# A hybrid decoder layer on one core: turned query and key rows split over all 128 partitions, and half of the second weight unit loaded into exponential tiles

## The chip, the core and the metric

The kernel runs on one core of one Trainium2 chip. The core has a matmul engine (PE, with its weight loads PEld), a vector engine (DVE), an activation engine (ACT), a general engine (POOL) and a queue that issues nearly all of this kernel's DMAs (SP). The metric is the device time of one launch in microseconds (us), lower is better; the median of several executions counts.

## What is computed

One decoder layer on x of 1 x 1024 x 1024 float32. The parts that matter here, shortened:

```python
h = rms_norm(x, norm1_w)
da_q, da_k, da_v, dn_qkv, dn_z, dn_a, dn_b = split(h @ w_in)
da_q = rms_norm(da_q.reshape(B, S, 4, 2, 64), q_norm_w)   # 4 heads, two maps of 64 each
da_k = rms_norm(da_k.reshape(B, S, 4, 2, 64), k_norm_w)
a = softmax(q1 @ k1.T) - lam * softmax(q2 @ k2.T)         # causal, per head
da_o = rms_norm(a @ v, da_out_norm_w) * (1 - lam_init)
dn_o = gated_delta_rule(conv_silu(dn_qkv), ...)           # 4 heads, chunked scan
x = x + concat(da_o, dn_o) @ w_out
x = x + square(relu(rms_norm(x, norm2_w) @ w_up)) @ w_down
```

## The kernel before the change

Every matmul of float32 data is made of two parts: a rounded high part (fp32r) and the low rest, and three products high x high, high x low, low x high. A weight block is therefore loaded as float32 (`raw`), rounded on ACT (L213) and its rest made on DVE (L214).

The launch runs in stages. To about 220 us come the first norm, the gate columns and the convolution stage of the DeltaNet heads. From there to about 620 us one stage mixes many streams: the blockwise inversion (`horner`), the chunked `scan` with its outputs (`scan_out`), the projections of the attention heads (`da_units`), the turning of normed queries and keys (`da_turns`), the attention itself (`scores`, `values`), the turning of its outputs and the output projection. Then the MLP runs to the end.

In the mixed stage the PE's order is written out by a planner (`Interleave`): every stream is a generator that says when its next piece can run by a table of costs (`act`, `vec`, `DMA_T`, `unit_time`), and the planner emits the piece of highest priority that is due. PE keeps that order to the letter. The order of ACT, DVE, POOL and SP is made by the tile framework's scheduler from the same program; each engine then works through its own list strictly in turn, and so does SP.

The pieces that the change and the prediction touch:

- `load_unit` (L199) loads one weight block after another. In the attention stage a half unit has four blocks, k = 0 to 3, of 128 x 512; each is two DMAs of 128 KB (L211), a rounding on ACT (L213) and a rest on DVE (L214). The float32 blocks go through a ring of two buffers (`wraw`), so the load of k = 2 stands behind the rest of k = 0.
- `da_units` (L987) has three units (512 columns each) by eight row tiles. A unit has two halves of the contraction, `kh` 0 and 1. Two row tiles share a turn: four k-groups of three matmuls (L1012 to L1014) for each tile with `kh` 0, then four for each with `kh` 1. The sums stand in two PSUM banks (`ps_qk`), one for each of the two tiles. `leave` drains a bank with one ACT instruction (`qn`, L1040; in the second unit L1034 and L1035). The next half unit's weights are loaded when the last pair has used the old ones, as the staged buffers `wH` and `wL` come in two pairs.
- `da_turns` (L956) turns 256 normed columns of one row tile: two PE transposes into `ps_qkt` (L965, L966), then high and low part. Partitions 0 to 63 of the turned tile hold the rows of map one, 64 to 127 those of map two. For each map m, ACT rounds the 64 partitions into `qa[a, m]` (L972) and DVE writes the rest into the other 64 partitions, `qa[b, m]` (L973). One DMA stores `qa` to `qk_d` (L977). There are 32 turns, two buffers of `qa`.
- `load_head` (L1064) loads a head's keys, one tile for each map (L1068), 512 KB each, 128 partitions. `load_q` (L1081) loads a query tile twice: `qa` as stored (L1085, 128 KB) and `qb` with the halves of the partitions exchanged (L1086, L1087, 64 KB each), so that two matmuls (L1148, L1149) give all four products of high and low parts.
- `horner` (L781) works in four tiles of the pool `ae` (tag `pexp`, four buffers): two named `gb`, two named `pb`. Later `scores` writes its exponentials into tiles of the same tag. DVE reads `gb` for the last time in the transposes behind L800.

What sets the order of the load of weights: the ring `wraw` for the raw blocks, the last reader of `wH` and `wL` on PE, and the place of each DMA on SP.

Of the kernel before, what the change touches and what calls it, by code (L numbers as in the profile page):

```python
# [9 lines left out]
F32 = mybir.dt.float32  # L10
# [109 lines left out]
def act(n, accum=False):  # L120
    return "S", 55.0 + 0.83 * n + (93.0 if accum else 0.0)


def vec(n, extra=0.0):
    return "V", 68.0 + 1.045 * n + extra
# [7 lines left out]
def tile_hymba_layer(  # L133
# [62 lines left out]
    hH = hpool.tile([P, KB, SEQ], F32R, name="hH")  # L196
    hL = hpool.tile([P, KB, SEQ], F32R, name="hL")

    def load_unit(src, ranges, k0=0, nk=KB, eng=None, rp=None):  # L199
        eng = eng or G  # L200
        width = sum(n for _, n in ranges)
        wh, wl = staged("wH"), staged("wL")
        wh = wh[:, :nk * width].rearrange("p (k c) -> p k c", k=nk)
        wl = wl[:, :nk * width].rearrange("p (k c) -> p k c", k=nk)
        st = 2 * UC // width
        for k in range(0, nk, st):
            raw = rp.tile([P, 2 * UC], F32, tag="wraw", name="wraw", bufs=5) if rp else laid("wraw")
            raw = raw[:, :st * width].rearrange("p (k c) -> p k c", k=st)
            o = 0
            for c0, n in ranges:  # L210
                nc.sync.dma_start(raw[:, :, o:o + n], src[:, k0 + k:k0 + k + st, c0:c0 + n])  # L211
                o += n
            S.copy(wh[:, k:k + st, :], raw)  # L213
            eng.tensor_tensor(wl[:, k:k + st, :], raw, wh[:, k:k + st, :].bitcast(F32), ALU.subtract)  # L214
        return wh, wl
# [552 lines left out]
    HF = (slice(0, 64), slice(64, 128))  # L768
    MM, TR = 219.0, 110.0

    def unit_time(eng="G", rate=1230.0):
        done = []
        for i in range(4):
            start = flow.now if i < 2 else done[i - 2]
            done.append(flow.chain(("S", 520.0), (eng, rate), start=start + DMA_T))
        return done

# [179 lines left out]
    def da_turns():  # L957
        for i in range(4 * NT):
            while not late:
                yield flow.now + 50, None  # L960
            g, kind, tb, qn, t = late[0]
            r = yield from flow.bank("px", at=max(t + 2000, qa_free[i % 2] - 500))
            late.pop(0)
            pt = px.tile([P, 512], F32, tag="px", name="ps_qkt")
            T.transpose(pt[:, 0:P], qn[:, 0:P], ident)  # L965
            T.transpose(pt[:, P:2 * P], qn[:, P:2 * P], ident)  # L966
            flow.begun(("qa", i % 2))
            qa = sd.tile([P, 2, 256], F32R, tag="qa", name="qa", bufs=2)
            wv = qw if kind == 0 else kw
            for m in range(2):  # L970
                a, b = HF[m], HF[1 - m]
                S.activation(qa[a, m, :], pt[a, 0:256], AF.Copy, scale=wv[a])  # L972
                V.scalar_tensor_tensor(qa[b, m, :], pt[a, 0:256], wv[a], qa[a, m, :].bitcast(F32),  # L973
                                       ALU.mult, ALU.subtract)
            flow.pe(2 * TR)
            t = flow.chain(act(256), act(256), vec(256, 60), vec(256, 60), start=max(flow.now, qa_free[i % 2]))
            flow.put_off(t, ("qa", i % 2), lambda g=g, kind=kind, tb=tb, qa=qa: nc.sync.dma_start(  # L977
                qk_d[g, kind, tb], qa.bitcast(F32).rearrange("p m (h t) -> p m h t", h=2)))
            qa_free[i % 2] = t + DMA_T
            flow.hold(r, t)  # L980
            state["turned"] += 1
            if state["turned"] % (2 * NT) == 0:
                flow.due(lambda t, key: key[0] == "qa")
                state["da"] += 1
                state["da_t"] = flow.now + 6000
        sdctx.close()
    def da_units():  # L987
        todo = [[(512, 256), (0, 256)], [(1024, 256), (768, 256)], [(1280, 256), (256, 256)]]

        def half_w(src, ranges, k0):  # L990
            return load_unit(src, ranges, k0, 4, eng=V), unit_time("V", 610.0)

        w = [(w, [0.0] * 4) for w in first_w]
        freed = [0.0, 0.0]
        for i in range(3):
            if i == 1:
                vts[0] = ap.tile([P, NT, P], F32, tag="vt", name="vt")
            for pair in range(NT // 2):
                pss = {}
                for kh in range(2):  # L1000
# [18 lines left out]
                            freed[j] = yield from leave(i, tb, ps)  # L1019
                    if pair == NT // 2 - 1:  # L1020
                        if i < 2:
                            w[kh] = half_w(w_in_v, todo[i + 1], 4 * kh)
                        elif kh == 0:
                            pre.append(half_w(w_out_v, [(0, 512)], 4))
        pctx.close()
# [38 lines left out]
    def load_head(h, pool):  # L1064
        KS = []
        for m in range(2):
            k = pool.tile([P, SEQ], F32R, tag=f"KS{m}", name=f"KS{m}")
            nc.sync.dma_start(k.bitcast(F32).rearrange("p (b t) -> p b t", t=P),  # L1068
                              qk_d[h // 2, 1, :, :, m, h % 2, :].rearrange("b p t -> p b t"))
            KS.append(k)  # L1070
        return KS

# [8 lines left out]
    def load_q(h, tb):  # L1081
        qa = ap.tile([P, 2, P], F32R, tag="qa", name="qa", bufs=2)
        qb = ap.tile([P, 2, P], F32R, tag="qb", name="qb", bufs=2)
        src = qk_d[h // 2, 0, tb, :, :, h % 2, :]
        nc.sync.dma_start(qa.bitcast(F32), src)  # L1085
        nc.sync.dma_start(qb[HF[0]].bitcast(F32), src[HF[1]])  # L1086
        nc.sync.dma_start(qb[HF[1]].bitcast(F32), src[HF[0]])  # L1087
        return qa, qb

    order = [(0, t) for t in range(NT)] + [(1, t) for t in range(NT)]  # L1090
# [764 lines left out]
```

## Time and profile before

| | |
|---|---|
| median of 3 runs | 1226.38 us (1225.47 to 1226.53) |
| the profiled execution's own time | 1226.58 us |
| its span, first to last instruction | 1224.9 us |
| PE busy | 1212.0 us, 99% of the span |
| DVE busy | 850.0 us, 69% |
| ACT busy | 604.6 us, 49% |
| mean granted clock of PE | 0.998 |

A row of a timeline gives start and duration in us, the engine, the line, the operation and its tiles, and in brackets the idle time of that engine ahead of it with what ended it. "PE busy" counts matmuls whose ends are modelled, so that a row's end may lie past the next row's start; the step from start to start is what a matmul costs. A row of a list of waits gives the total, how often, and the longest. A row by windows gives busy us of each engine in a stretch, and the granted PE clock as a share of full speed. SPq rows are DMA issues on the SP queue, not the transfers.

### The profile page before, as it was taken

The numbers are of one execution on the slowest core, as the hardware profiler recorded it, in microseconds if no ns is written. First come the engines' busy times: TensorE is split into PE (matmuls) and PEld (weight loads), VectorE is DVE, ScalarE is ACT, GpSimd is POOL, SyncE is SP. The second block draws the span as 40 slices with busy tenths as digits, with TensorE's granted clock in tenths as the row PEclk, the third lists the DMA queues.
The fourth block names the chain that finished last, engine by engine and source line by source line (L and its number), as shares of the span: only waits on it lengthen the run. The fifth ranks groups of instructions, "written<-read, shape, count | busy, mean of one in ns | idle before, by whom it ended". The sixth has DMA issues, their size and how long they took to land.

```text
span 1224.9 us, 17632 instructions
## 1 busy us (share of the span) xinstructions
PE 1212.0 (99%) x6330; PEld 1029.2 (84%) x6330; DVE 850.0 (69%) x1448; ACT 604.6 (49%) x1176; POOL 121.0 (10%) x162
## 2 busy tenths in 40 slices
PE   9999999999999999999999999999999999999998
PEld 9988888898888888888788888888888888888887
DVE  7786788477868577766798554566577955786553
ACT  8565545234556555656666444454554333333331
POOL 0011110223332230212100000000000000000000
PEclk9999999999999999999999999999999999999999
DMA  6564442456755584434528433443279855433301
GB/s 230 176 182 125 112 130 87 116 183 218 241 161 180 173 244 135 115 80 142 183 86 291 155 127 133 170 174 135 103 253 353 325 185 183 160 104 104 138 35 69
DMA packets 161087, 199.04 MB, mean 163 GB/s; under 512 B 21008, under 2 KB 120936, under 8 KB 161000
## 3 DMA queue, kind: packets, MB, share of 16 engines
q1 hardware_dynamic: 160856, 197.79, 49.3%
q8 instruction: 50, 0.82, 0.3%
q14 instruction: 37, 0.30, 0.1%
q10 hardware_dynamic: 144, 0.13, 0.0%
HBM read 132.32 MB, written 65.56 MB: 162 GB/s over the span
## 4 chain that ended last, share of the span: by engine, by line
PE 89%; DVE 4%; DMA 3%; ACT 2%; issue 1%; SPq 0%; POOL 0%; ACTq 0%; DVEq 0%
PE X L1454 5%; PE X L1453 5%; PE X L1452 5%; PE X L1768 4%; PE X L1769 4%; PE X L1770 4%; PE ps_dn L221 4%; PE ps_dn L219 4%; PE ps_dn L220 4%; PE ps_qk L1012 3%; PE Y L1454 3%; PE Y L1453 3%; PE Y L1452 3%; PE ps_qk L1014 3%; PE ps_qk L1013 2%; PE ps_o L1201 2%
## 5 line engine op out<-in xcount | busy, mean ns | idle before, releaser
L1371 ACT CAST hH<-ur 128x1024 fp32r<-128x1024 f32 x56 | 58.6, 1048 | 166.0 <-PE X L1769 79.7
L1372 DVE TENSOR_TENSOR hL<-ur,hH 128x1024 fp32r<-128x1024 f32 x56 | 68.5, 1224 | 79.8 <-ACT hH L1371 79.8
L1372 DVE TENSOR_TENSOR op<-raw,op 128x1024 fp32r<-128x1024 f32 x48 | 58.7, 1223 | 75.3 <-PE X L1453 42.3
L1768 PE MATMUL X<-hH 128*128 128x512 f32 x224 | 87.2, 389 | 0.0
L1769 PE MATMUL X<-hL,hH 128*128 128x512 f32 x224 | 87.2, 389 | 0.0
L1770 PE MATMUL X<-hH,hL 128*128 128x512 f32 x224 | 87.2, 389 | 0.0
L1012 PE MATMUL ps_qk<-wH,hH 128*128 128x512 f32 x192 | 82.2, 428 | 1.9 <-ACT qn L1040 1.9
L1014 PE MATMUL ps_qk<-wH,hL 128*128 128x512 f32 x192 | 75.8, 395 | 0.0
L219 PE MATMUL ps_dn<-hH,wH 128*128 128x512 f32 x192 | 75.7, 394 | 0.0
L220 PE MATMUL ps_dn<-hL,wH 128*128 128x512 f32 x192 | 75.6, 394 | 0.0
L1013 PE MATMUL ps_qk<-wL,hH 128*128 128x512 f32 x192 | 75.4, 393 | 0.1
L221 PE MATMUL ps_dn<-hH,wL 128*128 128x512 f32 x192 | 75.4, 393 | 0.0
L1372 DVE TENSOR_TENSOR hL<-dw,hH 128x1024 fp32r<-128x1024 f32 x56 | 68.2, 1220 | 3.2 <-ACT hH L1371 3.2
L1371 ACT CAST op<-raw 128x1024 fp32r<-128x1024 f32 x48 | 50.4, 1050 | 34.8 <-PE Y L1454 20.1
L1371 ACT CAST hH<-dw 128x1024 fp32r<-128x1024 f32 x56 | 58.6, 1047 | 16.7 <-DMA dw<-in_w_down_dram 5.1
L1157 ACT ACTIVATE pexp<-ps_sc,mx 128x128 f32<-128x128 f32 (+7 forms) x64 | 47.3, 740 | 26.1 <-DVE mx L1153 26.1
L595 DVE SCALAR_TENSOR_TENSOR cy<-cp,pv,cy 128x512 f32<-128x512 f32 x72 | 53.7, 750 | 7.8 <-ACT cy L593 7.0
L1153 DVE TENSOR_REDUCE mx<-ps_sc 128x1 f32<-128x128 f32 (+7 forms) x64 | 47.5, 754 | 14.1 <-PE ps_sc L1151 13.5
L1291 PE MATMUL ps_op<-wH,hH 128*128 128x512 f32 x128 | 53.6, 419 | 0.0
L1293 PE MATMUL ps_op<-wH,hL 128*128 128x512 f32 x128 | 50.3, 393 | 0.0
L1292 PE MATMUL ps_op<-wL,hH 128*128 128x512 f32 x128 | 50.0, 391 | 0.0
L1453 PE MATMUL Y<-hL,op 128*128 128x512 f32 x128 | 49.8, 389 | 0.0
(355 smaller groups left out, 3383.8 us busy)
## 6 DMA issues: line engine op xcount, KB each, us to landing
ur<-ud SPq DMA_DIRECT2D x28, 1024.0 KB, 4.9
raw<-in_w_up_dram SPq DMA_DIRECT2D x32, 512.0 KB, 3.7
dw<-in_w_down_dram SPq DMA_DIRECT2D x32, 512.0 KB, 7.2
qk_d<-qa SPq DMA_DIRECT2D x32, 256.0 KB, 3.1
ud<-ua SPq DMA_DIRECT2D x16, 512.0 KB, 4.0
ud<-s SPq DMA_DIRECT2D x16, 512.0 KB, 3.2
wraw<-in_w_in_dram SPq DMA_DIRECT2D x24, 256.0 KB, 3.5
wraw<-in_w_in_dram SPq DMA_DIRECT2D x48, 128.0 KB, 2.9
```

Source lines behind the costliest of these rows:

```text
L219: T.matmul(ps, lh(k), rh(k), start=(k == 0), stop=False)
L220: T.matmul(ps, lh(k), rl(k), start=False, stop=False)
L221: T.matmul(ps, ll(k), rh(k), start=False, stop=(k == n - 1))
L1012: T.matmul(ps, hH[:, 4 * kh + k, sl], wh[:, k, :], start=(kh + k == 0), stop=False)
L1013: T.matmul(ps, hH[:, 4 * kh + k, sl], wl[:, k, :], start=False, stop=False)
L1014: T.matmul(ps, hL[:, 4 * kh + k, sl], wh[:, k, :], start=False, stop=(kh + k == 4))
L1371: S.copy(dst[0], src)
L1372: V.tensor_tensor(dst[1], src, dst[0].bitcast(F32), ALU.subtract)
L1453: T.matmul(ps, op[0][:, k, cs], h[1][:, k, :], start=False, stop=False, skip_group_check=True)
L1768: T.matmul(o, v[0][:, j, sl], v[2][:, j, c], start=s0, stop=False, skip_group_check=True)
L1769: T.matmul(o, v[0][:, j, sl], v[3][:, j, c], start=False, stop=False, skip_group_check=True)
L1770: T.matmul(o, v[1][:, j, sl], v[2][:, j, c], start=False, stop=s1, skip_group_check=True)
```

## The change

Two things are changed. In `da_turns` one ACT instruction over 128 partitions writes the high part of all turned rows and one DVE instruction the rest, side by side in the free dimension, and the tile is stored so. The placing of high and low parts onto partition halves is done by the loads: `load_head` loads each key tile with two DMAs of 64 partitions, `load_q` loads `qa` and `qb` with two DMAs of 64 partitions each. And the half units of the second weight unit take a tile of the tag `pexp` each (`more`): blocks k = 2 and 3 land there, and only k = 0 and 1 use the ring. The planner's costs follow: a turn is one ACT and one DVE step in place of two each, and `unit_time` lets all four loads of such a half unit start at once.

```diff
--- before.py
+++ after.py
@@ -196,7 +196,7 @@
     hH = hpool.tile([P, KB, SEQ], F32R, name="hH")
     hL = hpool.tile([P, KB, SEQ], F32R, name="hL")
 
-    def load_unit(src, ranges, k0=0, nk=KB, eng=None, rp=None):
+    def load_unit(src, ranges, k0=0, nk=KB, eng=None, rp=None, more=None):
         eng = eng or G
         width = sum(n for _, n in ranges)
         wh, wl = staged("wH"), staged("wL")
@@ -204,7 +204,10 @@
         wl = wl[:, :nk * width].rearrange("p (k c) -> p k c", k=nk)
         st = 2 * UC // width
         for k in range(0, nk, st):
-            raw = rp.tile([P, 2 * UC], F32, tag="wraw", name="wraw", bufs=5) if rp else laid("wraw")
+            if more is not None and k > 1:
+                raw = more[:, 512 * (k - 2):512 * (k - 1)]
+            else:
+                raw = rp.tile([P, 2 * UC], F32, tag="wraw", name="wraw", bufs=5) if rp else laid("wraw")
             raw = raw[:, :st * width].rearrange("p (k c) -> p k c", k=st)
             o = 0
             for c0, n in ranges:
@@ -768,10 +771,10 @@
     HF = (slice(0, 64), slice(64, 128))
     MM, TR = 219.0, 110.0
 
-    def unit_time(eng="G", rate=1230.0):
+    def unit_time(eng="G", rate=1230.0, ring=2):
         done = []
         for i in range(4):
-            start = flow.now if i < 2 else done[i - 2]
+            start = flow.now if i < ring else done[i - 2]
             done.append(flow.chain(("S", 520.0), (eng, rate), start=start + DMA_T))
         return done
 
@@ -967,15 +970,12 @@
             flow.begun(("qa", i % 2))
             qa = sd.tile([P, 2, 256], F32R, tag="qa", name="qa", bufs=2)
             wv = qw if kind == 0 else kw
-            for m in range(2):
-                a, b = HF[m], HF[1 - m]
-                S.activation(qa[a, m, :], pt[a, 0:256], AF.Copy, scale=wv[a])
-                V.scalar_tensor_tensor(qa[b, m, :], pt[a, 0:256], wv[a], qa[a, m, :].bitcast(F32),
-                                       ALU.mult, ALU.subtract)
+            S.activation(qa[:, 0, :], pt[:, 0:256], AF.Copy, scale=wv)
+            V.scalar_tensor_tensor(qa[:, 1, :], pt[:, 0:256], wv, qa[:, 0, :].bitcast(F32), ALU.mult, ALU.subtract)
             flow.pe(2 * TR)
-            t = flow.chain(act(256), act(256), vec(256, 60), vec(256, 60), start=max(flow.now, qa_free[i % 2]))
+            t = flow.chain(act(256), vec(256, 60), start=max(flow.now, qa_free[i % 2]))
             flow.put_off(t, ("qa", i % 2), lambda g=g, kind=kind, tb=tb, qa=qa: nc.sync.dma_start(
-                qk_d[g, kind, tb], qa.bitcast(F32).rearrange("p m (h t) -> p m h t", h=2)))
+                qk_d[g, kind, tb], qa.bitcast(F32).rearrange("p x (h t) -> p x h t", h=2)))
             qa_free[i % 2] = t + DMA_T
             flow.hold(r, t)
             state["turned"] += 1
@@ -987,8 +987,8 @@
     def da_units():
         todo = [[(512, 256), (0, 256)], [(1024, 256), (768, 256)], [(1280, 256), (256, 256)]]
 
-        def half_w(src, ranges, k0):
-            return load_unit(src, ranges, k0, 4, eng=V), unit_time("V", 610.0)
+        def half_w(src, ranges, k0, more=None):
+            return load_unit(src, ranges, k0, 4, eng=V, more=more), unit_time("V", 610.0, 2 if more is None else 4)
 
         w = [(w, [0.0] * 4) for w in first_w]
         freed = [0.0, 0.0]
@@ -1019,7 +1019,8 @@
                             freed[j] = yield from leave(i, tb, ps)
                     if pair == NT // 2 - 1:
                         if i < 2:
-                            w[kh] = half_w(w_in_v, todo[i + 1], 4 * kh)
+                            more = ae.tile([P, SEQ], F32, tag="pexp", name="more") if i == 0 else None
+                            w[kh] = half_w(w_in_v, todo[i + 1], 4 * kh, more)
                         elif kh == 0:
                             pre.append(half_w(w_out_v, [(0, 512)], 4))
         pctx.close()
@@ -1065,8 +1066,9 @@
         KS = []
         for m in range(2):
             k = pool.tile([P, SEQ], F32R, tag=f"KS{m}", name=f"KS{m}")
-            nc.sync.dma_start(k.bitcast(F32).rearrange("p (b t) -> p b t", t=P),
-                              qk_d[h // 2, 1, :, :, m, h % 2, :].rearrange("b p t -> p b t"))
+            kv = k.bitcast(F32).rearrange("p (b t) -> p b t", t=P)
+            for x in range(2):
+                nc.sync.dma_start(kv[HF[x]], qk_d[h // 2, 1, :, HF[m], x, h % 2, :].rearrange("b p t -> p b t"))
             KS.append(k)
         return KS
 
@@ -1081,10 +1083,10 @@
     def load_q(h, tb):
         qa = ap.tile([P, 2, P], F32R, tag="qa", name="qa", bufs=2)
         qb = ap.tile([P, 2, P], F32R, tag="qb", name="qb", bufs=2)
-        src = qk_d[h // 2, 0, tb, :, :, h % 2, :]
-        nc.sync.dma_start(qa.bitcast(F32), src)
-        nc.sync.dma_start(qb[HF[0]].bitcast(F32), src[HF[1]])
-        nc.sync.dma_start(qb[HF[1]].bitcast(F32), src[HF[0]])
+        parts = [qk_d[h // 2, 0, tb, :, x, h % 2, :].rearrange("(m r) t -> r m t", m=2) for x in range(2)]
+        for t, swap in ((qa, 0), (qb, 1)):
+            for x in range(2):
+                nc.sync.dma_start(t[HF[x]].bitcast(F32), parts[x ^ swap])
         return qa, qb
 
     order = [(0, t) for t in range(NT)] + [(1, t) for t in range(NT)]
```

The planner and the scheduler move instructions after this. Line numbers of the changed kernel are higher by 3 from line 207 to the turns and by 0 to 2 behind them.

First place, ACT around the end of the first attention unit. `wH` with a number is the staged weight of a half unit of the second one (`kh` 0, then `kh` 1); `qn` are the drains of the projection banks, `qa` the high parts of turned rows, `osq` squares in the scan's outputs. Before:

```order
L972 ACTIVATE qa<-ps_qkt,pv 64x256 x2
L972 ACTIVATE qa<-ps_qkt,qw 64x256
L213 CAST wH_3476<-wraw 128x512 x2
L972 ACTIVATE qa<-ps_qkt,qw 64x256
L1040 ACTIVATE qn<-ps_qk,rt 128x512
L213 CAST wH_3476<-wraw 128x512 x2
L972 ACTIVATE qa<-ps_qkt,pv 64x256
L972 ACTIVATE qa<-ps_qkt,qw 64x256
L972 ACTIVATE qa<-ps_qkt,pv 64x256
L919 ACTIVATE osq,so<-oc,small_73 128x128
L1040 ACTIVATE qn<-ps_qk,rt 128x512
L213 CAST wH_3619<-wraw 128x512
```

And now:

```order
L922 ACTIVATE osq,so<-oc,small_73 128x128 x2
L216 CAST wH_3459<-wraw 128x512 x2
L216 CAST wH_3459<-more 128x512 x2
L973 ACTIVATE qa<-ps_qkt,pv 128x256
L973 ACTIVATE qa<-ps_qkt,qw 128x256
L1041 ACTIVATE qn<-ps_qk,rt 128x512 x2
L216 CAST wH_3566<-wraw 128x512 x2
L216 CAST wH_3566<-more 128x512 x2
L922 ACTIVATE osq,so<-oc,small_73 128x128 x4
```

The four roundings of a half unit now stand together ahead of the last two drains of the first unit; before, two of them stood between these drains.

Second place, SP from the end of `horner` to the same point. `pka` and `pkb` are the scan's inputs, `zgt` and `mixn_d` belong to its outputs. Before, the first loads of the second unit in this stage:

```order
L839 DMA pka<-park_d 128x384 x4
L977 DMA qk_d<-qa 128x512
L211 DMA wraw<-in_w_in_dram 128x256 x4
L977 DMA qk_d<-qa 128x512
L894 DMA pkb<-park_d 128x256 x3
L211 DMA wraw<-in_w_in_dram 128x256 x4
L894 DMA pkb<-park_d 128x256
```

Now eight of them stand much earlier on the queue, ahead of the scan's third chunk:

```order
L897 DMA pkb<-park_d 128x256
L214 DMA more<-in_w_in_dram 128x256 x3
L842 DMA pka<-park_d 128x384 x4
L214 DMA more<-in_w_in_dram 128x256 x5
L897 DMA pkb<-park_d 128x256 x4
```

The first of them waits for the last readers of the `gb` tiles, on PE and DVE; the four that remain at the old place are blocks 0 and 1 of `kh` 1.

Third place, PE at the border of the two units. `ps_qk` with a number is one row tile's bank, `wH1`/`wL1` the second half of the first unit, `wH0`/`wL0` the first half of the second; L864 (now L867) and L912 (now L915) are steps of the scan and its outputs. Before:

```order
L864 MATMUL ps_A_2558<-sr_3546,lt_1793 128x128
L1012 MATMUL ps_qk_3421<-wH1_2492,hH_101 128x512
L1013 MATMUL ps_qk_3421<-wL1_2493,hH_101 128x512
L1014 MATMUL ps_qk_3421<-wH1_2492,hL_102 128x512
L1012 MATMUL ps_qk_3642<-wH0_3476,hH_101 128x512
L1013 MATMUL ps_qk_3642<-wL0_3477,hH_101 128x512
```

And now:

```order
L1014 MATMUL ps_qk_3377<-wH1_2492,hL_102 128x512
L1012 MATMUL ps_qk_3587<-wH0_3459,hH_101 128x512
L1013 MATMUL ps_qk_3587<-wL0_3460,hH_101 128x512
L1014 MATMUL ps_qk_3587<-wH0_3459,hL_102 128x512
L867 MATMUL ps_A_2558<-sr_3495,lt_1075 128x128
L867 MATMUL ps_A_2558<-sr_3497,lt_1237 128x128
L867 MATMUL ps_A_2558<-sr_3499,lt_1633 128x128
L867 MATMUL ps_A_2558<-sr_3501,lt_1793 128x128
L915 MATMUL ps_o2_3602<-sy_2556,pkb_3442 128x128
```

In both, the bank that is finished here (3421, now 3377) is needed again, drained, for the second row tile of the new unit. Before, the four k-groups of the first row tile follow one another directly up to that point, 12 matmuls of 512 columns; now the scan's steps L867, L915 and L878, four matmuls each, stand between them.

## The prediction

> **What bounds the kernel now.** I read the table of engines first, then the shares of the chain that ended last. This is the page:
>
> ```profile
> PE 1212.0 (99%) x6330; PEld 1029.2 (84%) x6330; DVE 850.0 (69%) x1448; ACT 604.6 (49%) x1176; POOL 121.0 (10%) x162
> PE 89%; DVE 4%; DMA 3%; ACT 2%; issue 1%; SPq 0%; POOL 0%; ACTq 0%; DVEq 0%
> ```
>
> PE is busy for 99% of the span and makes 89% of the chain. The change leaves PE's work alone, so it can gain only what PE loses to waits or to a lowered clock. The second view is the list of PE's waits (total us, how often, longest):
>
> ```profile
> PE ps_qk L1012 <- ACT qn L1040: 1.9, 1, 1.9
> PE ps_sc L1148 <- ACT pexp L1157: 1.4, 2, 0.9
> PE ps_tr L1384 <- DVE hL L257: 1.1, 1, 1.1
> PE ps_at L1189 <- DVE pexp L1167: 1.0, 1, 1.0
> ```
>
> One wait stands out, at the border of the first two attention units. PE's timeline there:
>
> ```profile
> 303.73 0.40 PE L1014 MATMUL ps_qk<-wH,hL 128*128 128x512 f32 x1
> ...
> 308.79 0.50 PE L1012 MATMUL ps_qk<-wH,hH 128*128 128x512 f32 x1 [1.91 <-ACT qn L1040]
> ...
> 310.39 0.63 PE L1014 MATMUL ps_qk<-wH,hL 128*128 128x512 f32 x1
> ```
>
> PE wants the bank of row tile 7 about 2.8 us after its last product there (from 303.73 + 0.40 to 308.79 - 1.91 = 306.9), and waits 1.91 us for ACT's drain. Behind the wait the same matmul takes 0.63 us in place of 0.40. Third, the windows (length; busy us of PE, PEld, DVE, ACT, POOL; granted clock; DMA share; GB/s):
>
> ```profile
> 300.00:310.00 10.00, 8.09 (x46) 6.63 (x45) 6.56 (x16) 4.86 (x12) 2.32 (x3) 0.98 0.68 220
> 310.00:320.00 10.00, 10.00 (x53) 8.88 (x52) 9.74 (x27) 5.32 (x14) 4.16 (x4) 0.85 0.76 228
> ```
>
> The clock lost is 10 x (1 - 0.98) + 10 x (1 - 0.85) = 1.7 us. Fourth, why the drain was late, from the timelines of SP, DVE and ACT:
>
> ```profile
> 297.27 1.29 DVE L214 TENSOR_TENSOR wL<-wraw,wH 128x512 fp32r<-128x512 f32 x2
> 297.99 1.96 SPq L211 DMA_DIRECT2D wraw<-in_w_in_dram  x4
> 303.87 1.34 ACT L213 CAST wH<-wraw 128x512 fp32r<-128x512 f32 x2 [4.86 <-DMA wraw<-in_w_in_dram]
> 305.12 0.47 ACT L972 ACTIVATE qa<-ps_qkt,pv 64x256 fp32r<-64x256 f32 x1
> 306.81 0.47 ACT L972 ACTIVATE qa<-ps_qkt,pv 64x256 fp32r<-64x256 f32 x1 [0.87 <-DVE qa L973]
> 307.53 0.40 ACT L919 ACTIVATE osq<-oc,small 128x128 f32<-128x128 f32 x1 [0.25 <-DVE oc L914]
> 308.05 0.69 ACT L1040 ACTIVATE qn<-ps_qk,rt 128x512 f32<-128x512 f32 x1
> ```
>
> Blocks 2 and 3 of the second unit may be loaded only when DVE has read blocks 0 and 1 out of the ring (297.27). Their loads are issued from 297.99, ACT meets their rounding at 303.87 after 4.86 us of idleness, and behind it, in ACT's order, stand the turns and the drain that PE waits for.
>
> **The change part by part.** *Blocks 2 and 3 in `more`.* In the changed order the roundings of `kh` 0 no longer stand behind a transfer: their loads stand on SP near the end of `horner`, and the buffers come free with
>
> ```profile
> 245.10 0.70 DVE L802 STREAM_TRANSPOSE lt<-gb 128x512 f32<-128x512 f32 x1
> ...
> 248.48 0.70 DVE L802 STREAM_TRANSPOSE lt<-gb 128x512 f32<-128x512 f32 x1
> ```
>
> at 245.8 (the first `gb`) and 249.2, some 45 us before the rounding. SP gets a new wait by it: it waits there for these buffers, and behind it are queued the scan's next inputs:
>
> ```profile
> 247.13 2.57 SPq L839 DMA_DIRECT2D pka<-park_d  x4
> ...
> 259.24 1.16 PE L905 MATMUL ps_o<-S,pkb 128*128 128x128 f32 x8
> ```
>
> Three of the loads stand ahead of `pka`: from 245.8 they end near 247.4, 0.3 after it was issued before. Five stand ahead of `pkb`: with 4 x 0.5 for `pka` and 5 x 0.5 for themselves they end near 252, 7 us before the first matmul on `pkb`. I cost this at nothing, the cover being those 7 us; were the loads held to 249.2, `pkb` would come 3 us later and still be in time. The rows of the tile `wraw` price what is left:
>
> ```profile
> L213 ACT CAST wH<-wraw x16: 606/621/632, 295.3 to 387.5; 128x512 fp32r<-128x512 f32 x16
> DMA to landing us min/median/max: 2.1/3.8/5.2
> ```
>
> All four roundings are 4 x 0.62 = 2.5 us of ACT and may run when PE has let go of the old `wH`, about 5 us before 303.87. Tile 7's bank now has 5.4 us of PE work between its last product and its reuse (2.8 before); tile 6's has 2.8 (5.9 before), and its drain stands behind the four roundings and two turns. (Such times of PE work are counted in the changed order with the durations of the rows.) I take the wait away whole, **-1.9** (bounds 0 and -1.9), and the clock's loss that followed it, **-1.7** (0 and -1.7). The Trainium skill ("TensorE: Matmul & The Clock Gate", Why this matters for your kernels) warns of PE idle gaps above about 3 us as what halves the clock. By it a wait of 1.91 us costs no clock, and the sum would be 1.7 higher; the row at 310.39 shows the lower clock behind this wait all the same, so the measurement decides. Late next is the wait of the first value products for DVE's `pexp` (L1189, 1.0 in the list above): with DVE relieved it may go or stay, 0 to -1.0; I take **-0.4**, nearer to staying, since its rows belong to the scores and not to the turns.
>
> *The turns.* Rows of the tile `qa`:
>
> ```profile
> L972 ACT ACTIVATE qa<-ps_qkt,pv x32: 456/469/472, 261.5 to 393.9; 64x256 fp32r<-64x256 f32 x32
> L973 DVE SCALAR_TENSOR_TENSOR qa<-ps_qkt,pv,qa x32: 476/482/490, 262.5 to 395.7; 64x256 fp32r<-64x256 f32 x32
> ```
>
> These are the rows of one kind of turn; with the other there are 64 of each engine, and 32 go. For 128 partitions by 256 no row exists. 128x128 takes 0.40 on ACT (L919 at 307.53) and 128x512 takes 0.69 (L1040 at 308.05), so 128x256 lies between, about 0.50: the duration follows the free size and hardly the partitions. So ACT loses 32 x 0.47 = 15.0 us and DVE 32 x 0.48 = 15.4 us, less 32 x 0.03 = 1 us for the longer instructions that stay. PE waits for neither in the long run, so this is worth nothing by itself. What it shortens is a turn's chain: the two ACT steps of one turn lie 306.81 - 305.12 = 1.69 us apart, and that distance goes.
>
> *The loads.* DMA issues (KB, median us to landing):
>
> ```profile
> qa<-qk_d SPq DMA_DIRECT2D x32, 128.0 KB, 2.6
> qb<-qk_d SPq DMA_DIRECT2D x64, 64.0 KB, 2.8
> KS<-qk_d SPq DMA_DIRECT2D x8, 512.0 KB, 5.3
> ```
>
> For the tile `KS` alone, and then the two tightest loads with the scores that need them:
>
> ```profile
> DMA to landing us min/median/max: 4.3/5.3/6.3
> ```
>
> ```profile
> 329.13 1.00 SPq L1068 DMA_DIRECT2D KS<-qk_d  x2
> 333.64 0.31 PE L1148 MATMUL ps_sc<-KS,qa 128*128 128x128 f32 x1
> ...
> 406.75 0.59 SPq L1087 DMA_DIRECT2D qb<-qk_d  x1
> 410.39 0.34 PE L1148 MATMUL ps_sc<-KS,qa 128*128 128x384 f32 x1
> ```
>
> There are 32 + 8 more issues, about 40 x 0.55 = 22 us of SP's time over some 300 us; SP is 0% of the chain. The first score starts 4.5 us after its keys are issued, 0.2 above the shortest landing; one more issue of 0.5 is in front, and the turn's 1.69 us are saved: nothing. The queries of the score at 410.39 are issued last at 406.75 and land by 409.55 (2.8 later), 0.84 ahead. A fourth issue takes 0.56 of that, and the changed order has 4.4 us of PE work where 4.8 stood between the buffer's release and the score. Between 0 and 0.6 is lost; I take **+0.3**. A rule speaks against these halves. The Trainium skill ("SBUF — State Buffer", Can I just issue two DMAs to hit both halves?) says that two transfers at partitions 0 and 64 serialize, with only 6% over one. The rows agree in part: 64 KB take 2.8 where 128 KB take 2.6, so halving the bytes made nothing faster. By that rule the keys come later and the time is that of the first rival, 1226.0 in place of 1223.0.
>
> *The order.* PE takes up scores some us earlier, and two steps of the scan stand closer behind the steps that they wait for (about 1.4 and 1.6 us of PE work, where the smallest was 1.6). Between 0 and 0.9 us of small waits; I take **+0.3**, by the number of places.
>
> The sum is -1.9 - 1.7 - 0.4 + 0.3 + 0.3 = -3.4. From the execution's own 1226.58 (span 1224.9 and 1.7 around it), 0.2 above the median of 1226.38, it gives 1223.2, or **1223.0** against the median. 0.2%, about what a measurement of this kernel can tell from no change, is 2.45 us: faster is below 1223.93, slower above 1228.83.
>
> **The rivals.** *Halves land late.* If the second half of the keys lands half a transfer later (5.3 / 2 = 2.65), the first score has 0.5 + 2.65 against the 1.69 saved and the 0.2 to spare: 1.3 us of waiting. The second score loses some 0.3, the score at 410 its full 0.6 instead of 0.3; a wait like that at 306.9 would bring its 1.7 of clock as well. That is +1.9 to +3.6 on the sum, 1224.9 to 1226.6, and I put it at 1226.0. For it speaks that 64 KB are no faster than 128 KB; against it, that the halves of `qb` are already loaded so and no wait is shown for them. *DVE becomes the bound behind 460 us (slower).* Scores come earlier in PE's order, and the work of 90 us there is packed into some 81:
>
> ```profile
> 460.00:550.00 90.00, 88.97 (x553) 79.13 (x552) 64.65 (x129) 51.88 (x131) 13.64 (x19) 1.00 0.38 110
> ```
>
> DVE goes from 64.65 / 90 = 72% to 64.65 / 81 = 80%, and a score's values follow it after 9 to 13 us of PE work instead of 12 to 18. If each of the twenty units there waits 0.3 us, that is +6, so 1229.0. It decides when these waits pass 3.4 + 2.45 = 5.9 us. Against it: 80% leaves DVE room, and the distances are still several times one score's chain. *The relief helps more (faster).* With 15 us less on ACT and on DVE, half of the other waits listed above (1.4, 1.1, and the 0.6 of 1.0 not yet taken) go too: -1.6 more, 1221.4. *The change doesn't do what it says.* The wait only moves to tile 6's bank, whose 2.8 us must hold what is left of the roundings, two turns and a drain: 2.5 + 2 x 0.5 + 0.7. If they can't start early, neither the wait nor the clock is won, and the rest of the sum, +0.2, gives 1226.6.
>
> **How the numbers follow.** The forecast has 0.52, with its own range 1222.2 (the pexp wait and no new ones) to 1224.4 (half of the new waits at their upper end and part of the stall left). Late halves 0.22, DVE's bound 0.11, the greater relief 0.11, nothing done 0.04. Faster is four fifths of the forecast and the greater relief, 0.42 + 0.11 = 0.53. Slower is DVE's bound and a tail of the late halves, 0.12. The rest, 0.35, is within 0.2%. The range goes from 1220.7, beyond the greater relief, to 1227.7, beyond the late halves; DVE's bound and little else lie outside.
>
> **What would show it.** Right: no wait of L1012 near 307 us, no idle time of ACT for `wraw` at 299 to 304, a full clock in both windows, 32 turns of one ACT row near 0.50 and one DVE row near 0.48. Wrong: a wait at the first score or near 410 of over 0.6 us (late halves), many waits of value products behind 460 us (DVE), or a wait for `qn` that is still there under tile 6's name.

## The result, and the profile after

The changed kernel is slower: a median of 1230.28 us over six executions (1226.58 to 1232.84) beside 1226.05 for the kernel before, a ratio of 1.0032 with a 95% interval of 1.0018 to 1.0046. The executions of the kernel before lie within 1.3 us of each other, those of the changed one within 6.3. The profiled execution of the changed kernel is its fastest, 1226.58 us with a span of 1224.9, so what it shows is the smaller part of the loss. Two later profiles of the same kernel, 1229.49 and 1233.10 us, show the rest.

First what was forecast to go. The same windows as before (length; busy us of PE, PEld, DVE, ACT, POOL; granted clock; DMA share; GB/s), and one more:

```profile
300.00:310.00 10.00, 10.00 (x60) 8.72 (x59) 7.81 (x22) 5.29 (x15) 5.66 (x6) 1.00 0.74 231
310.00:320.00 10.00, 10.00 (x59) 8.65 (x58) 6.62 (x21) 2.79 (x7) 4.08 (x5) 1.00 0.64 213
400.00:410.00 10.00, 7.94 (x39) 6.52 (x38) 4.91 (x18) 4.08 (x14) 0.55 (x1) 0.84 0.72 199
```

The stall at the border of the units is gone, with its clock: PE is busy throughout both windows and the clock is full. ACT's timeline there, where 4.86 us of idleness for a transfer stood before:

```profile
294.03 1.14 ACT L216 CAST wH<-wraw 128x512 fp32r<-128x512 f32 x2 [1.00 <-PE ps_qk L1014]
295.08 1.13 ACT L216 CAST wH<-more 128x512 fp32r<-128x512 f32 x2
296.12 0.46 ACT L973 ACTIVATE qa<-ps_qkt,pv 128x256 fp32r<-128x256 f32 x1
297.62 0.47 ACT L973 ACTIVATE qa<-ps_qkt,qw 128x256 fp32r<-128x256 f32 x1 [1.03 <-PE ps_qkt L969]
299.07 0.69 ACT L1041 ACTIVATE qn<-ps_qk,rt 128x512 f32<-128x512 f32 x1 [0.98 <-PE ps_qk L1014]
301.79 0.69 ACT L1041 ACTIVATE qn<-ps_qk,rt 128x512 f32<-128x512 f32 x1 [2.03 <-PE ps_qk L1014]
```

Now none of the four roundings waits for a transfer, and both drains wait for PE and no longer PE for them. A turn is one ACT row of 0.46 to 0.47 us, not the 0.50 that I took.

The third window is a new loss of the same kind. The list of PE's waits in the first profile of the changed kernel (total, how often, longest):

```profile
PE ps_sc L1150 <- DMA qa<-qk_d: 2.0, 1, 2.0
PE ps_sc L1150 <- ACT pexp L1159: 2.0, 3, 0.9
PE ps_sc L1151 <- DMA qb<-qk_d: 1.8, 1, 1.8
PE ps_at L1191 <- DVE ri L1166: 1.5, 1, 1.5
```

Two scores wait for their queries, the one at 405 for `qa` and the one at 508 for `qb`; neither wait stood in the list of before. By the median the transfers take what they took before (DMA issues: KB, median us to landing):

```profile
qa<-qk_d SPq DMA_DIRECT2D x64, 64.0 KB, 2.9
qb<-qk_d SPq DMA_DIRECT2D x64, 64.0 KB, 2.3
KS<-qk_d SPq DMA_DIRECT2D x16, 256.0 KB, 5.0
```

But a median hides single transfers, and the two waits have different causes. At 405 it is the landing that comes late. Counted from the first one on, the queries of this score are the eleventh, issued at 399.10 (SP's rows, then PE's, then the landing of the tile `KS`):

```profile
397.13 0.58 SPq L1071 DMA_DIRECT2D KS<-qk_d  x1
...
399.10 1.23 SPq L1089 DMA_DIRECT2D qa<-qk_d  x2
...
405.49 0.41 PE L1150 MATMUL ps_sc<-KS,qa 128*128 128x384 f32 x1 [2.03 <-DMA qa<-qk_d]
DMA to landing us min/median/max: 3.8/5.0/7.6
```

The second half of `qa` is issued at about 399.7, and PE goes on when it has landed, at about 405.4: 5.7 us later, where the median is 2.9. Two microseconds ahead of these queries stand the last keys of the third head, whose first score comes only at 468; a transfer of keys takes up to 7.6 us here. In the kernel before, some 6 us lay between the last of these keys and the same queries, and those landed in time for the score at 410.39:

```profile
398.89 1.04 SPq L1068 DMA_DIRECT2D KS<-qk_d  x2
...
405.49 0.54 SPq L1085 DMA_DIRECT2D qa<-qk_d  x1
```

At 508 it is the issue that comes late. SP's timeline ahead of the wait, and PE's at it:

```profile
503.32 0.33 SPq L1220 DMA_DIRECT2D mixa_d<-om  x1
503.74 0.57 SPq L1089 DMA_DIRECT2D qa<-qk_d  x1
504.41 0.54 SPq L214 DMA_DIRECT2D wraw<-in_w_out_dram  x1
505.00 0.57 SPq L1089 DMA_DIRECT2D qa<-qk_d  x1
505.67 0.54 SPq L214 DMA_DIRECT2D wraw<-in_w_out_dram  x1
506.31 1.22 SPq L1089 DMA_DIRECT2D qb<-qk_d  x2
```

```profile
508.05 0.38 PE L1150 MATMUL ps_sc<-KS,qa 128*128 128x320 f32 x1
510.23 0.41 PE L1151 MATMUL ps_sc<-KS,qb 128*128 128x320 f32 x1 [1.80 <-DMA qb<-qk_d]
```

The four issues of one query tile begin when SP is done with a store of an attention output (503.32), and with two weight loads between them they last to 507.53, that is 3.8 us, and the score needs the last of them at 508. The kernel before, for the same score (SP's timeline, then PE's):

```profile
504.00 0.53 SPq L1085 DMA_DIRECT2D qa<-qk_d  x1
504.62 0.56 SPq L1086 DMA_DIRECT2D qb<-qk_d  x1
505.24 0.59 SPq L1087 DMA_DIRECT2D qb<-qk_d  x1
```

```profile
511.70 0.39 PE L1148 MATMUL ps_sc<-KS,qa 128*128 128x320 f32 x1
```

Its three issues took 1.8 us in one piece, and the score came 5.9 us behind the last of them. The buffer sets the start too. There are two buffers for queries, and the one for this tile comes free with the scores two tiles earlier: before, their last matmul on it started at 503.81, 7.9 us ahead of the score at 511.70; now it starts at 502.55, 5.5 us ahead of the score at 508.05, and SP's store holds the first issue about 1 us longer. In the profile of 1233.10 us the same two places wait longer:

```profile
PE ps_sc L1150 <- DMA qa<-qk_d: 2.7, 1, 2.7
PE ps_sc L1151 <- DMA qb<-qk_d: 2.6, 1, 2.6
```

### The profile page after: what moved, and what is told of

It reads as the page before. It is cut to its first block, busy times and chain, and to the rows that moved or that the text cites. A ratio compares the mean times of both kernels' runs of the same rounds, so it can differ in the third digit from the quotient of the medians.

```text
span 1224.9 us, 17610 instructions
## 1 busy us (share of the span) xinstructions
PE 1210.4 (99%) x6330; PEld 1028.7 (84%) x6330; DVE 829.5 (68%) x1416; ACT 589.7 (48%) x1144; POOL 124.1 (10%) x162
## 4 chain that ended last, share of the span: by engine, by line
PE 92%; DMA 3%; DVE 2%; issue 2%; ACT 1%; POOL 1%; SPq 1%; ACTq 0%; POOLq 0%
PE X L1455 5%; PE X L1454 5%; PE X L1456 5%; PE X L1772 4%; PE X L1770 4%; PE X L1771 4%; PE ps_dn L224 4%; PE ps_dn L222 4%; PE ps_dn L223 4%; PE ps_qk L1012 3%; PE ps_qk L1014 3%; PE ps_qk L1013 3%; PE Y L1455 3%; PE Y L1454 3%; PE Y L1456 3%; PE Z L1772 2%
## 5 line engine op out<-in xcount | busy, mean ns | idle before, releaser
L1454 PE MATMUL Y<-hH,op 128*128 128x512 f32 x128 | 49.8, 389 | 0.0
```

The source lines that it names most:

```text
L1454: T.matmul(ps, op[0][:, k, cs], h[0][:, k, :], start=start and k == 0, stop=False, skip_group_check=True)
```

## The experiments

Theory 1: the split loads cost the time, by the fourth issue of a query tile, by the halves of the keys, or by both. Theory 2: the order of PE costs it, in which scores come earlier than their queries can. There are sixteen runs, in four groups on four chips. The kernel before ran beside each group on the same chip, and its median moved from one to the next (1225.3 to 1226.6 us), so ratios are compared and not times. The diffs are shortened.

| kernel | PE's order | loads of a query tile / a head's keys | ratio to before | interval |
|---|---|---|---|---|
| changed (after_again) | changed | 4 / 4 | 1.0037 | 1.0024 to 1.0050 |
| changed (after_third) | changed | 4 / 4 | 1.0034 | 1.0022 to 1.0047 |
| slow_turn | as before from 440 us | 4 / 4 | 1.0015 | 1.0006 to 1.0024 |
| halved_q4k4 | changed | 4 / 4 | 1.0017 | 1.0008 to 1.0026 |
| halved_q4 | changed | 4 / 2 | 1.0008 | 0.9999 to 1.0016 |
| halved_q112 | changed | 4 / 2 | 1.0004 | 0.9996 to 1.0013 |
| halved_k4 | changed | 3 / 4 | 0.9991 | 0.9983 to 1.0000 |
| halved | changed | 3 / 2 | 0.9980 | 0.9971 to 0.9988 |
| halved_slow | as slow_turn | 3 / 2 | 0.9987 | 0.9978 to 0.9996 |
| om_pool | changed | 4 / 4 | 0.9986 | 0.9977 to 0.9995 |
| halved_om | changed | 3 / 2 | 0.9975 | 0.9965 to 0.9984 |
| before_om | before | 3 / 2 | 1.0001 | 0.9992 to 1.0010 |
| more_only | as slow_turn | 3 / 2 | 1.0004 | 0.9996 to 1.0013 |
| more_early | changed | 3 / 2 | 1.0016 | 1.0007 to 1.0026 |
| turns_halved | its own to 440 us | 3 / 2 | 1.0018 | 1.0009 to 1.0027 |
| placed2 | changed | 3 / 2 | 1.0733 | 1.0719 to 1.0748 |

**after_again, after_third** (the changed kernel again).

> The changed kernel once more, for a second profile and more executions. If late queries set its time, another execution shows the same scores waiting, for other lengths (in the first profile 2.0, 1.8 and some of 0.3 us): waits for qa, qb or KS of 4 us and more in an execution of 1229 or more. If its executions differ by something else (waits for ACT or DVE, the clock without a wait), the profile shows that. Time: 1226 to 1233, median near 1230.

> The changed kernel on the same chip as the other three, to compare halved_q4k4 with it: a ratio of 1.0025 to 1.005, and again waits for queries near 405 and 510.

The medians were 1230.74 and 1230.19 us. The same scores wait in each profile, for different lengths, as expected: 2.0 and 1.8, then 2.2 and 2.4, then 2.7 and 2.6 us.

**placed2** placed the rows by the stores, and tells nothing of the loads:

```diff
-nc.sync.dma_start(qk_d[g, kind, tb], qa.bitcast(F32).rearrange("p x (h t) -> p x h t", h=2))
+[nc.sync.dma_start(qk_d[g, kind, tb][HF[x]].rearrange("r m h t -> m r (h t)"), qa[:, x, :].bitcast(F32))
+ for x in range(2)]
```

> The turns and the loads into exponential tiles stay as in the changed kernel, and PE's order is the changed one to the letter. Only the placing moves: each turn stores its high rows and its low rows with one DMA each (64 stores in place of 32) to the places that the kernel before used, so a query tile is again loaded with three DMAs and a head's keys with two. Theory 1 (the fourth DMA of each query load and the halves of keys cost the time): the queries land about 0.6 to 2 us sooner, the waits of scores for qa and qb (3.8 us in the changed kernel's profile) go, and the time is 1221 to 1224 us. Theory 2 (the earlier order of the scores costs it, whatever the loads are): the waits stay within 1 us of what they were, 1228 to 1231. Theory 3 (only both together): 1224 to 1226.

It took 1316.82 us. The tile `qa` shows why: ACT waits for the stores in 13 places, and its waits come to 65.6 us.

```profile
  DMA qk_d<-qa: 65.6, 13
```

**halved** cuts the stores the other way, rows first, and takes the loads of the kernel before:

```diff
+[nc.sync.dma_start(qk_d[g, kind, tb].rearrange("(x r) m h t -> m r x (h t)", x=2)[m], qa[HF[m]].bitcast(F32))
+ for m in range(2)]
```

> The placing by the stores once more, since the run placed2 told nothing of the loads (its stores of 128 KB took 2.7 us each, one after the other). Each turn now stores the 64 partitions of map one and the 64 of map two with one DMA each, rows first, so 64 stores in place of 32; a query tile is again loaded with three DMAs and a head's keys with two. PE's order is the changed one to the letter. Theory 1 (the fourth DMA and the halves of the loads cost the time): 1224 to 1227 us, and the waits for qa near 406 and for qb near 510 (2.4 and 2.6 us in the second profile of the changed kernel) are gone or below 0.5. Theory 2 (the earlier order of the scores): these waits stay above 1 us, those for pexp and ri near 366 and 372 (1.0 and 1.7) stay too, 1228.5 to 1231 us.

It took 1223.77 us: theory 1. PE's order is the changed one to the letter, yet no wait for `qa` or `qb` is left in its list, while those for `pexp` and `ri` are still there, as in the changed kernel:

```profile
PE ps_sc L1150 <- ACT pexp L1159: 2.8, 3, 1.0
PE ps_at L1191 <- DVE ri L1166: 2.0, 1, 2.0
```

The same score as above, now at 507.64, has its queries in time, from three issues that last 2.4 us with one weight load between them:

```profile
502.97 0.54 SPq L1087 DMA_DIRECT2D qa<-qk_d  x1
...
504.24 0.52 SPq L1088 DMA_DIRECT2D qb<-qk_d  x1
504.82 0.59 SPq L1089 DMA_DIRECT2D qb<-qk_d  x1
```

At the other place the last keys are issued at 394.11 and the queries at 401.98, 7.9 us later, and nothing waits.

**slow_turn, halved_slow** cost a turn as two steps of each engine, which puts PE's order back:

```diff
-t = flow.chain(act(256), vec(256, 60), start=max(flow.now, qa_free[i % 2]))
+t = flow.chain(act(256), act(256), vec(256, 60), vec(256, 60), start=max(flow.now, qa_free[i % 2]))
```

> The changed kernel with one line of the planner as before: a turn is costed as two steps of ACT and two of DVE, though it is one of each. The instructions and the split loads are those of the changed kernel; PE's order behind 440 us is again that of the kernel before, with scores up to 11 us later. Theory 1 (the split loads): the split loads still come late, 1227 to 1230 us. Theory 2 (the order): the queries have the margins of before again (0.3 us at the least, mostly 2 to 10), no wait of a score for qa or qb above 0.5 us, and 1221 to 1224 us. Theory 3 (both together): 1222 to 1225.

> As the kernel halved, and the planner costs a turn as two steps of each engine, as before, so that PE's order is that of slow_turn and more_only. Beside slow_turn (1227.85) it shows what the split loads cost in the late order: theory 1 says 1224 to 1226, theory 2 says within 1 us of slow_turn. Beside halved it shows what the order costs with whole loads: theory 1 says within 1 us of it, theory 2 says 2 to 4 us less.

With split loads the earlier order costs about 0.2% (1.0034 and 1.0037 beside 1.0015, with intervals that barely touch; the first measurement, 1.0032, has one that overlaps more). With whole loads it costs nothing: 0.9980 beside 0.9987, with intervals that overlap. So theory 2 is false by itself, and true as a multiplier: an earlier score turns later queries into a wait. In the later order the split still costs 1.0015 beside 0.9987; slow_turn's profile has two waits for `qb` left, the longer 0.9 us.

**more_only, more_early** are the kernel before with the exponential tiles, and with the planner's costs of before or after:

> The kernel before with the second part of the change alone: blocks 2 and 3 of the second unit in exponential tiles and the planner's ring of four; turns, stores and loads of queries and keys are those of before. PE's order is that of the kernel slow_turn. All theories say that the wait at 306.9 us (1.9) and the lower clock behind it (1.7) go and that no load of queries comes late: 1222 to 1223.5 us. If the time is 1225 or more, the gain of this part is not what I take it for.

> The kernel before with the second part of the change (more_only, 1227.48) and one number of the planner: a turn is costed as one step of each engine, though it is two. Turns, stores and loads are those of before; PE's order is the changed one to the letter. Theory 1 (the split loads): about as more_only, 1226.5 to 1228.5. Theory 2 (the order): 2 to 4 us above more_only, 1229.5 to 1232, with waits of scores near 406 and 510 although each query tile is loaded with three DMAs.

more_only gained nothing (1227.48 us), against every theory. Its wait at 306.9 is gone, and 6 us later stands this one, with a granted clock of 0.83 behind it:

```profile
314.49 0.30 PE L968 MATMUL ps_qkt<-ident,qn 128*128 128x128 f32 x1 [2.48 <-DVE qa L976]
```

```profile
310.00:320.00 10.00, 7.52 (x29) 5.86 (x29) 8.80 (x23) 5.70 (x17) 3.71 (x4) 0.83 0.54 165
```

The old turn, two steps of each engine in ping-pong behind the roundings, is late next. more_early (1227.77 us) shows no wait for queries above 0.2 us in this early order, which again speaks against theory 2. Its ratio is 0.0012 above that of more_only, with intervals that overlap, so that the order may cost a little here by other waits.

**turns_halved** is the other half: halved without the exponential tiles.

```diff
-more = ae.tile([P, SEQ], F32, tag="pexp", name="more") if i == 0 else None
+more = None
```

> The kernel halved without the loads into exponential tiles (all four blocks go through the ring again); the planner's cost for the ring goes with them, so PE's order differs from it between 300 and 440 us. It shows what that part of the change is worth beside cheap turns: if the wait near 307 and its lower clock come back, 3 to 4 us above halved, 1.0005 to 1.001. If cheap turns alone remove that wait, 0.998.

It took 1228.5 us, 1.0018, more than expected and 0.38% above halved. The ring's wait is back on ACT, and with it a wait of PE for the roundings, now for the last block of the second unit's `kh` 1 at 317.70, nine microseconds behind the old place:

```profile
317.03 0.62 ACT L216 CAST wH<-wraw 128x512 fp32r<-128x512 f32 x1 [2.88 <-DMA wraw<-in_w_in_dram]
```

```profile
PE ps_qk L1013 <- ACT wH L216: 2.5, 1, 2.5
```

So the exponential tiles, with the order that the planner makes of them, are worth some 4.7 us (0.0038 x 1226) beside cheap turns and nothing without them (more_only): with either part alone a stall of about 2.5 us stands within ten microseconds of the old one. Not all of the 4.7 us is that stall. The order to 440 us is another one here, and turns_halved has a second wait, of 1.9 us at 395.7 for a turn, with a clock of 0.83 in its window, that halved hasn't, while it lacks halved's wait for `ri`.

**om_pool, before_om, halved_om** move the stores of the attention outputs from SP's queue to POOL's:

```diff
-flow.put_off(t, ("om", turn_no[0] % 2), lambda h=h, tb=tb, om=om: nc.sync.dma_start(
+flow.put_off(t, ("om", turn_no[0] % 2), lambda h=h, tb=tb, om=om: nc.gpsimd.dma_start(
```

> The changed kernel with one word changed: the attention outputs (mixa_d from om) are stored from the queue of POOL and no longer from SP. In the changed kernel the queries of the score at 508 are issued from 503.7 on, right behind a store of om that SP had waited for (503.32), and the score waits 1.8 to 2.6 us for their last quarter. If waiting in line on SP makes the queries late: these queries are issued 2 to 4 us earlier, the wait near 510 goes with the lower clock behind it, and the time falls by 2 to 4 us, to 1226.5 to 1228.5. If it is the transfers or the buffers that are late: 1229.5 to 1231.5.

> The kernel before with the stores of om on POOL's queue and nothing else: a control. If om_pool gained because the changed kernel's queries stood behind these stores, it gains nothing here, 1225.5 to 1227, since no score of the kernel before waits for its queries. If the stores cost time on SP in any kernel: 1222 to 1224.

> The kernel halved with the stores of om on POOL's queue, as in om_pool. If the split loads cost time only by waiting in line on SP, the two remedies mend the same waits and do not add: 1222.5 to 1224. If each mends waits of its own, 1220 to 1222.

om_pool keeps every split and takes 0.9986 (1223.96 us, less than either side expected); the control before_om stays at 1.0001. The wait for `qb` near 510 is gone from its list and one of 1.3 us for `qa`, at the other place, is left:

```profile
PE ps_sc L1150 <- DMA qa<-qk_d: 1.3, 1, 1.3
```

The queries of the score at 508 (now 508.27) were expected 2 to 4 us earlier. Their first issue came 0.8 us earlier, and the last ended at 506.15 in place of 507.53, with one weight load between them in place of two:

```profile
502.98 0.57 SPq L1089 DMA_DIRECT2D qa<-qk_d  x1
...
504.91 1.24 SPq L1089 DMA_DIRECT2D qb<-qk_d  x2
```

SP issued nothing between 498.8 and 502.98: the buffer held these queries, whose last earlier matmul starts at 502.79. A third buffer was not tried. So four issues cost little where these stores are out of SP's line: at 508 it is the line that costs the time, on top of the buffer. halved_om is the fastest kernel, 1221.89 us and 0.9975, but its interval overlaps that of halved: the two remedies mend mostly the same waits.

**halved_q4, halved_q112, halved_k4, halved_q4k4** put the splits back one at a time:

```diff
-nc.sync.dma_start(qa.bitcast(F32), src)
+for x in range(2):                                  # halved_q112: slices 0:112 and 112:128
+    nc.sync.dma_start(qa[HF[x]].bitcast(F32), src[HF[x]])
```

> The kernel halved (1223.77) with one edit: the query tile qa is loaded with two DMAs of 64 partitions in place of one of 128, so a query tile takes four issues again; keys stay at two DMAs for a head. If the queries carry the loss of the changed kernel: 1227 to 1231, with waits for qa near 406 and qb near 510. If the halves of the keys carry it: 1223 to 1225.

> As halved_q4, but qa is cut into 112 and 16 partitions: four issues, and nearly the whole tile in one transfer. If it is the fourth issue on SP that makes the queries late, it is as slow as halved_q4 within 1.5 us. If it is the transfer of 64 partitions (two halves that serialize), it is near halved, 1223 to 1225.

> The kernel halved (ratio to before 0.9980) with the keys of a head in four DMAs of 64 partitions in place of two; a query tile stays at three. What is open: the fourth issue of the queries brought 0.9980 to 1.0008 (halved_q4), the changed kernel has 1.0037. If the keys' halves hold the rest by themselves: 0.9995 to 1.001. If the eight issues more cost nothing without the fourth of the queries: 0.997 to 0.999.

> Both splits on top of halved: the loads are those of the changed kernel in number, form and size, and only the stores differ (two of 64 partitions in place of one of 128). If the loads explain the whole of the changed kernel's loss: a ratio of 1.003 to 1.005, as the changed kernel. If the two stores of a turn gain something by themselves: near 1.001, and the rest is the stores'.

The fourth issue raises 0.9980 to 1.0008, about 3.4 us, and it does nearly the same when the extra transfer has 16 partitions (1.0004, with an interval that overlaps and lies above that of halved): it is the count, not the 64 partitions. In the profile of halved_q4, its slowest execution, the waits for queries are back at both places; that of halved_q112, a faster one, has 0.8 us for `qb` and none for `qa`. The rows of halved_q4:

```profile
PE ps_sc L1152 <- DMA qb<-qk_d: 2.3, 2, 2.0
PE ps_sc L1151 <- DMA qa<-qk_d: 1.9, 1, 1.9
```

The wait for `qa` at 405 is there with whole keys, which are issued 3.9 us ahead of the queries (395.08 and 398.93); `qa` lands 5.8 us after its issue. So it needs no halves of keys, only keys close in front. That their transfers hold up the queries is read from the traces; no run moved the keys alone.

The keys' halves add 0.0011, some 1.3 us, an effect at the edge of its interval, and both together 0.0037. The changed kernel lies a further 0.0015 to 0.0020 above halved_q4k4, about 2 us, with intervals that overlap. Whether the single store of a turn, or where its place on SP leaves the loads, costs these 2 us was not settled.

## Why the prediction was wrong

The forecast was 1223.0, with a range to 1227.7 and a chance of 0.12 for slower; 1230.28 was measured. Point by point, by its own steps:

- *The stall at 306.9* (-1.9) and *its clock* (-1.7): right. Both are gone in every profile of the changed kernel. The reason was only half told. Blocks 2 and 3 in `more` take this wait away, but alone they win no time, as more_only shows: a turn of two steps becomes the next stall.
- *The first value products* (-0.4): the 1.0 us is gone whole. But new waits of the same kind came, which *the order* (+0.3) had to cover: near 372 for `ri` (1.5 to 1.9) and near 366 for `pexp` (0.7 to 1.0). Together they are 2.2 to 2.7 us in the changed kernel's profiles, and about 4.6 in halved, where a clock of 0.83 follows the longer one (below); I had put 0.3. They stand in halved too, so they are not what sets the changed kernel apart from it; which smaller waits of before went to make up for them was not traced.
- *SP at the end of horner* (nothing): right. The first loads went out at 245.39, `pkb` at 252.11, and no product waited for it there:

```profile
245.39 1.28 SPq L214 DMA_DIRECT2D more<-in_w_in_dram  x3
...
252.11 2.06 SPq L897 DMA_DIRECT2D pkb<-park_d  x4
```

- *The turns* (nothing by themselves): right in cost, 0.47 us each.
- *The loads* (+0.3, "between 0 and 0.6"): this is the step that failed. The runs put the split at about 4.5 us (0.9980 to 1.0017) and up to 6.6 us (0.9980 to 1.0034, with the single store of a turn in it). I priced two places out of 32, and only the wait of one more issue. The place at 410 was the right one, but I let the queries land in the 2.8 us of the median. They were issued when their buffer was free, as before, and the last half took 5.7 us (6.0 and 6.5 in the later profiles), with keys 2 us in front of it. The wait was 2.0 to 2.7 us, with a clock of 0.84 behind it in two profiles of three. The place at 508 was not looked at: in the order of before its queries were issued 7.7 us ahead of it, at 504.00 for a score at 511.70; in the changed order the first issue stays at 503.74, held by the buffer and then by SP's line, the last of four ends at 507.53, and the score has moved to 508.05. The wait was 1.8 to 2.6 us. I had counted that the scores move earlier, and asked this of DVE alone. I wrote that 22 us of issues on SP cost nothing since "SP is 0% of the chain". That share says that nothing waited for SP yet, not how much would.
- *The sum without that term* was 1222.7; the kernel without the splits, halved, takes 0.9980, which is 1223.9 beside the 1226.38 used there.

Of the rivals, *halves land late* came nearest, in its place and by its consequence (a lowered clock). It was given +1.9 to +3.6 on top of a sum that holds +0.3, where the runs show 4.5 to 6.6 in all. Its mechanism is borne out in part. At 405 the queries did land late, but not for being halves: a whole tile of keys in front does it too (halved_q4), the medians of halves and whole tiles are alike, and om_pool, which keeps all halves, recovered the loss. By the Trainium skill ("SBUF — State Buffer", Can I just issue two DMAs to hit both halves?) two halves serialize; the cut of 112 and 16 partitions cost nearly what the cut of 64 and 64 did. At 508 it was the issue. *DVE becomes the bound* is not borne out: over the ninety microseconds from 450 DVE is busy for 66.71 us, 74%, and PE for 88.20. Nor is *the relief helps more*: of the waits it named, the 1.1 became 0.8 and those for `pexp` went from 1.4 to 2.0. *The change doesn't do what it says* is refuted by the first point: no wait for `qn` is left.

```profile
450.00:540.00 90.00, 88.20 (x553) 78.54 (x552) 66.71 (x131) 54.37 (x133) 14.37 (x19) 1.00 0.49 130
```

## What to carry to other kernels

An engine that is 0% of the critical chain is free only as long as the margins of what it issues stay: when an order moves its consumers earlier, work out for each transfer how long before its reader it is issued, and count what bounds it: when its buffer comes free, what stands in front of it on the issuing queue, and which large transfers are issued just ahead of it. A median time to landing does not price the last of these. Extra DMA issues are priced by the tightest of those margins, and one wait of 2 us on PE can bring a lowered clock along. Two changes that each take away one of two stalls, one close behind the other, can win nothing apart (1.0004 and 1.0018 here) and something together (0.9980); try them together before judging either.

## What the runs showed of the hardware

- A store of 128 KB written as [2, 64, 256] (placed2) was slow: ACT waited 65.6 / 13 = 5.0 us at each place for a buffer to be stored. The same bytes written as [64, 2, 256] (halved) landed in 2.5 us by the median, and ACT's waits for them came to 3.4 us in 3 places. Why the store with the outermost two was slow was not tried. The row of halved:

```profile
qk_d<-qa SPq DMA_DIRECT2D x64, 128.0 KB, 2.5
```

- The lower clock did not follow the length of a wait alone. It came behind 2.03 us at 405 in the changed kernel's first profile (0.84) and behind the 2.0 us for `ri` in halved (0.83), but not behind the 2.2 us for `qa` at 406 in the profile of 1229.49 us. The windows of halved, and then those of after_again:

```profile
370.00:380.00 10.00, 8.02 (x39) 6.89 (x38) 7.90 (x18) 6.82 (x17) 3.52 (x4) 0.83 0.33 91
```

```profile
400.00:410.00 10.00, 7.75 (x49) 6.57 (x49) 4.71 (x16) 4.84 (x18) 0.55 (x1) 1.00 0.79 207
410.00:420.00 10.00, 10.00 (x59) 8.70 (x58) 6.17 (x21) 5.83 (x18) 4.36 (x6) 1.00 0.51 146
```

By the Trainium skill ("TensorE: Matmul & The Clock Gate", Why this matters for your kernels) gaps above about 3 us lower the clock; here shorter ones sufficed. In the profiles of all kernels but placed2, between 255 and 620 us, a lower clock came behind six of the fifteen waits of PE between 1.8 and 2.2 us and behind all five of 2.4 to 2.7 us. What else decides was not tried.
